# FFN input chunks in pairs by seven half products, and the next layer's tables and modulation in its own phases

## The chip, the cores and the metric

The kernel runs on one core of one Trainium2 chip. The metric is the time of the whole program on the device in microseconds (us), as the median of its runs. A separate execution, taken by the hardware profiler, gives the trace.

## The reference

Two layers of a trunk over 640 tokens (512 latent, 128 context) of width 1024, all float32. Each layer has two halves, of which the second is the one whose products change:

```python
def swiglu(xn, w_ffn_in, w_ffn_out):
    gu = xn @ w_ffn_in
    g, u = gu[..., :D_FF], gu[..., D_FF:]
    return (jax.nn.silu(g) * u) @ w_ffn_out

def layer(x, cond, lp, ctx, rope_cs):
    sh_m, sc_m, g_m, sh_f, sc_f, g_f = modulation(cond, lp['w_ada'], lp['b_ada'])
    xn = rms_norm(x, lp['norm_mix_g']) * (1 + sc_m) + sh_m
    mix, ckv_n, k_pe, ssm_final = mixer(xn, lp, ctx, rope_cs)
    x = x + g_m * mix
    xn = rms_norm(x, lp['norm_ffn_g']) * (1 + sc_f) + sh_f
    x = x + g_f * swiglu(xn, lp['w_ffn_in'], lp['w_ffn_out'])
    return x, ckv_n, k_pe, ssm_final
```

D_FF is 2816, so w_ffn_in is 1024 by 5632. The modulation is silu(cond) @ w_ada + b_ada, six sections of 1024 channels, for two streams (latent and context), and depends on no token. The mixer's state-space branch needs tables (powers, kernels, rotations) that depend only on the layer's parameters.

## The kernel before

**Layout.** Activations stand channel-major: 8 tiles of 128 channels by 640 tokens, in two halves of 320. Every operand of a float32 product is split in a high and a low part (fp32r), and a product is three matmuls: high weights by high activations, low by high, high by low. A chunk of weights is 128 input channels by 8 tiles (kt) of 128 output columns, 512 KB; `weights` loads it (tile `wraw`), ScalarE casts it to `whi` (L319), the vector engine subtracts to make `wlo` (L320). There are three buffers of each of these (`WBUFS`), and loads and splits are put 400 instructions ahead in priority.

**Stages of a layer.** `mixer_in` (input projection, attention, Fourier, convolution), `mixer_out` (state-space branch and gated merges; its last results are the tiles `acc`, split into `xh` and `xl`), and `tail`: the output projection with the residual and the norm, then the FFN. In the FFN a tile f of 128 hidden channels takes a gate chunk and an input chunk (in the code `wfi[f]` and `wfi[NF+f]`, NF = 22), each 8 x 3 x 2 = 48 matmuls of 320 columns, all by `mm` (L238). Silu of the gate is on ScalarE (L1521), the multiplication with the other chunk on the vector engine (L1523), and the result f_s is split in `hh` and `hl`. FFN_ROUNDS cuts the 22 tiles in rounds of 8, 8 and 6; after each round 8 output chunks (`wfo`) add its part to the residual (L1332). The last three chunks of the last round go by halves of the tokens, so that the norm (squares at L433) can start early. One further tile of the next round stands ahead of each output projection.

**Layer 1's work in layer 0.** During `tail` of layer 0 two side chains run: `layer_tables` (the state-space tables of layer 1, then the rotations) and `modulations` of all six sections of layer 1. The latter reads each 512 KB of `w_ada` with the vector engine, two operations of 1024 columns (one for each stream, L572) for a tile. For layer 0 itself the tables are made in `mixer_in`, the rotations beside its attention, and four sections of its modulation in `mixer_out`.

**Order.** TensorE's order is fixed when the program is written: a main stream of products, and between them the steps of side chains, each put where an estimated clock (`now`) says that it is ready. The other engines' orders come from a scheduler with priorities; `issue_after(anchor)` ties the modulation's operations to the main stream's progress on the vector engine. Sums are collected in PSUM: the tile `main` has two buffers of two banks, one bank for each half of the tokens.

Of the kernel before, what the change touches and what calls it, by code (L numbers as in the profile page):

```python
# [9 lines left out]
F32 = mybir.dt.float32  # L10
# [30 lines left out]
TABLES_PACE = (1.5, 3.0)  # L41
TABLES_START = 80.0
ROT_START, ROT_PACE = 8.0, 6.0
MOD_START = (12.0, 90.0)
MOD_PACE = (10.5, 7.0)
# [5 lines left out]
# ---------------------------------------------------------------- host layout  # L51
# [12 lines left out]
def _constants():  # L64
# [17 lines left out]
    # the DFT over the latent positions p = 8k + s: sums and differences of the positions p and -p come in (those of  # L82
    # 0 and 256 share a place), a half of the positions goes out, the even ones first
# [16 lines left out]
    # the sum over four 32-row blocks of the rotary key, and of its swap  # L100
# [27 lines left out]
    # the first two sections of the first layer: piece t holds the tiles t of both,  # L128
    # [half of the channels, channel, 4 x 2 x 128]; the others: [channel of the section, channel]
# [75 lines left out]
# ---------------------------------------------------------------- the program  # L205
class Program:
    def __init__(self, tc, A, O, taps=None):
        self.tc, self.nc, self.A, self.O, self.taps = tc, tc.nc, A, O, taps or {}
        self.n = 0
        self.now = 0.0             # estimated time of the tensor engine, in ns  # L210
        self.ntags = (("hh", 9), ("hl", 9))
# [3 lines left out]
        self.spare = 0             # chunks of weights to come that the vector engine has no time for  # L215
        self.anchor = None         # the last step of the main stream on the vector engine
        self.slots = [[False, 0.0] for _ in range(2)]

# [12 lines left out]
    # -- the order of the tensor engine: a main stream of products, and between its parts the  # L231
    # steps of side chains, each put where its operands are expected to be ready
# [11 lines left out]
    def side(self, gen, urgent=False, behind=False):  # L244
        """Starts a side chain: a generator that yields the time (us) until its next step is ready."""
# [16 lines left out]
    def tick(self):  # L262
        """Runs the side steps that are ready."""
# [74 lines left out]
    def main_ps(self):  # L338
        return self.t(self.ps, [128, 2, 512], "main", bufs=2)
# [1263 lines left out]
```

## Time and profile before

| what | value |
|---|---|
| median of 3 runs | 2672.55 us (2671.49 to 2681.19) |
| span of the profiled execution | 2683.6 us |
| TensorE busy | 2618.7 us (98%) |
| vector engine (DVE) busy | 1534.2 us (57%) |
| ScalarE (ACT) busy | 883.2 us (33%) |
| GpSimd (POOL) busy | 187.9 us (7%) |
| chain that ended last | TensorE 84%, issue 9%, vector engine, ScalarE and DMA 2% each |

Busy shares are of the span. The chain is followed back from the last instruction: at each step to what released it. PE is TensorE, PEld its loading of weights, SP the engine that issues most loads. PEclk is the granted clock of TensorE, 1.00 being 2.4 GHz and 0.50 being 1.2 GHz.

### The profile page before, as it was taken

What the parts mean: (1) busy time and instruction counts of PE and PEld (TensorE: products, weight loads), DVE (VectorE), ACT (ScalarE), POOL (GpSimd) and SP (SyncE); (2) the same over time, 40 slices, a digit from 0 to 9 for tenths busy, and PEclk for the clock granted to TensorE, in tenths of its full rate; (3) what the DMA queues carried; (4) which work ended last, traced back from release to release, by engine and by line L of the source; (5) the groups of instructions that cost most, each with busy time, mean ns of one, the idle gap of its engine ahead of it and who ended that gap; (6) DMA issues with size and microseconds to landing.
All of it is one profiled execution on the core that took longest, in us unless ns stands there. A gap on an engine that the chain in (4) does not pass through costs nothing.

```text
span 2683.6 us, 44723 instructions
## 1 busy us (share of the span) xinstructions
PE 2618.7 (98%) x18518; PEld 2505.7 (93%) x18518; DVE 1534.2 (57%) x3061; ACT 883.2 (33%) x1393; POOL 187.9 (7%) x316
## 2 busy tenths in 40 slices
PE   7999999999999999999999899999999999999999
PEld 5987898999999899999979779999999999999999
DVE  5888764776557579989453356654454444232323
ACT  5334544233224422221243244433323233212211
POOL 0110000111001100000020000011100010000000
PEclk8999999999999999999999999999999999999999
DMA  6442115574435255655232221155532322222222
GB/s 250 135 150 85 56 61 173 176 216 140 126 121 172 63 165 181 202 179 166 80 119 75 60 63 52 50 155 160 149 99 80 107 74 71 79 72 79 71 75 75
DMA packets 118747, 312.78 MB, mean 117 GB/s; under 512 B 35344, under 2 KB 46160, under 8 KB 118288
## 3 DMA queue, kind: packets, MB, share of 16 engines
q1 hardware_dynamic: 99376, 250.52, 30.7%
q0 software_dynamic: 16432, 55.39, 6.1%
q10 hardware_dynamic: 2736, 4.01, 0.4%
q8 instruction: 146, 2.39, 0.4%
q14 instruction: 57, 0.47, 0.1%
HBM read 267.07 MB, written 42.80 MB: 115 GB/s over the span
## 4 chain that ended last, share of the span: by engine, by line
PE 84%; issue 9%; DVE 2%; ACT 2%; DMA 2%; POOL 0%; ACTq 0%; SPq 0%; DVEq 0%; POOLq 0%
PE main L238 74%; PE side L238 9%; PE side L242 1%; DMA s_EF<-d_et 1%; DVE xl L463 1%; DVE wlo L320 0%; ACT whi L319 0%; ACT pq L897 0%; DVE hl L458 0%; ACT P L794 0%; DMA yb<-d_br 0%; POOL d_r L1136 0%; DVE hh L458 0%; DVE sm L791 0%; ACT xh L461 0%
## 5 line engine op out<-in xcount | busy, mean ns | idle before, releaser
L238 PE MATMUL main<-xh,whi 128*128 128x320 f32 x3488 | 831.2, 315 | 1.7 <-ACT xh L461 1.3
L238 PE MATMUL main<-xl,whi 128*128 128x320 f32 x3488 | 815.8, 311 | 1.7 <-DVE xl L463 1.5
L238 PE MATMUL main<-xh,wlo 128*128 128x320 f32 x3488 | 813.5, 310 | 0.0
L319 ACT CAST whi<-wraw 128x1024 fp32r<-128x1024 f32 (+1 forms) x302 | 312.3, 1034 | 1162.4 <-PE main L238 675.9
L238 PEld LDWEIGHTS main<-xh,whi 128*128 128x128 f32 x3488 | 585.7, 189 | 25.1 <-issue 19.9
L238 PEld LDWEIGHTS main<-xl,whi 128*128 128x128 f32 x3488 | 590.4, 189 | 6.7 <-DVE xl L463 6.4
L320 DVE TENSOR_TENSOR wlo<-wraw,whi 128x1024 fp32r<-128x1024 f32 (+1 forms) x302 | 367.7, 1218 | 397.0 <-ACT whi L319 395.7
L238 PEld LDWEIGHTS main<-xh,wlo 128*128 128x128 f32 x3488 | 590.5, 189 | 0.0
L238 PE MATMUL main<-yb,whi 128*128 128x320 f32 x1152 | 231.3, 312 | 2.1 <-ACT yb L319 2.1
L572 DVE SCALAR_TENSOR_TENSOR ada_j<-ada,ada_c 128x1024 bf16<-128x1024 f32 x160 | 195.1, 1219 | 3.8 <-DMA ada<-wada 2.9
L238 PEld LDWEIGHTS main<-yb,whi 128*128 128x128 f32 x1152 | 184.7, 189 | 3.0 <-ACT yb L319 2.4
L1332 DVE SCALAR_TENSOR_TENSOR x<-main,ada,x 128x320 f32<-128x320 f32 (+2 forms) x192 | 75.6, 434 | 177.2 <-PE main L238 176.9
L238 PE MATMUL main<-hh,whi 128*128 128x320 f32 x704 | 167.4, 311 | 0.0
L238 PE MATMUL main<-hh,wlo 128*128 128x320 f32 x704 | 166.2, 309 | 0.0
L238 PE MATMUL main<-hl,whi 128*128 128x320 f32 x704 | 166.2, 309 | 0.0
L238 PE MATMUL main<-yb,wlo 128*128 128x320 f32 x576 | 131.9, 310 | 0.0
L1523 DVE TENSOR_TENSOR f_s<-main,f_s 128x640 f32<-128x640 f32 x44 | 36.2, 824 | 150.6 <-PE main L238 150.6
L238 PEld LDWEIGHTS main<-hh,whi 128*128 128x128 f32 x704 | 119.0, 188 | 3.5 <-issue 3.5
L238 PEld LDWEIGHTS main<-hh,wlo 128*128 128x128 f32 x704 | 119.2, 188 | 0.0
L238 PEld LDWEIGHTS main<-hl,whi 128*128 128x128 f32 x704 | 119.2, 188 | 0.0
L238 PEld LDWEIGHTS main<-yb,wlo 128*128 128x128 f32 x576 | 97.1, 189 | 0.0
L794 ACT ACTIVATE P<-side,sm,rq 128x640 f32<-128x640 f32 (+1 forms) x80 | 63.9, 800 | 98.7 <-DVE sm L792 97.0
(320 smaller groups left out, 2761.3 us busy)
## 6 DMA issues: line engine op xcount, KB each, us to landing
ada<-wada SPq DMA_DIRECT2D x96, 512.0 KB, 4.4
wraw<-wfi SPq DMA_DIRECT2D x88, 512.0 KB, 3.6
wraw<-wgate SPq DMA_DIRECT2D x64, 512.0 KB, 3.6
wraw<-win SPq DMA_DIRECT2D x50, 512.0 KB, 3.7
wraw<-wbr SPq DMA_DIRECT2D x32, 512.0 KB, 3.7
wraw<-wfo SPq DMA_DIRECT2D x32, 512.0 KB, 3.6
d_f<-t_G POOLq DMA_DIRECT2D x16, 512.0 KB, 4.1
d_et<-t_et POOLq DMA_DIRECT2D x16, 512.0 KB, 5.1
```

The costliest lines, as they stand in the source:

```text
L238: self.nc.tensor.matmul(out, lhsT, rhs, **kw)
L242: self.nc.tensor.transpose(out, in_, ident)
L319: self.nc.scalar.copy(out=hi, in_=src)
L320: self.nc.vector.tensor_sub(out=lo, in0=src, in1=hi.bitcast(F32))
L463: nc.vector.scalar_tensor_tensor(out=xl[:, a:b], in0=t[:, a:b], scalar=B[:, s:s + 1], in1=xh.bitcast(F32)[:, a:b], op0=ALU.add, op1=ALU.su ...
L572: nc.vector.scalar_tensor_tensor(out=junk, in0=w, scalar=1.0, in1=sc[:, s, :], op0=ALU.mult, op1=ALU.mult, accum_out=self.ada[l][:, o + t, ...
L794: nc.scalar.activation(out=p[:, :nk].rearrange("p (a b) -> p a b", a=s.shape[1]), in_=s, func=AF.Exp, scale=rq, bias=small[:, 1:2], accum_ ...
L1332: self.anchor = nc.vector.scalar_tensor_tensor(out=x[:, o:o + n], in0=p, scalar=gcol[:, s:s + 1], in1=x[:, o:o + n], op0=ALU.mult, op1=ALU ...
L1523: self.anchor = nc.vector.tensor_mul(out=two(s), in0=pu[:, :, :HALF], in1=two(s))
```

## The change

**Pairs.** The tiles f = 0 and 1 of each layer stay as they were. From f = 2 on (`PLAIN`) the gate chunk and the input chunk are computed together as a 2 x 2 product: columns gate and input, channels in two halves of four tiles (kt), tokens in two halves. In place of eight half products there are seven (Strassen's scheme in Winograd's form), of 4 x 3 = 12 matmuls each. Four of them take sums of weight halves, made for each pair on the vector engine in `wsum` and then split, and four take sums of activations, T1 to T4, made once per layer by `sums` after f = 0 from copies of the normed tiles (tiles `bs`), T1 being written over an operand by `place` at f = 2. A pair takes four `whi` and four `wlo` buffers (seven halves of 512 columns), still out of three. The order is P1, P2, P5, U2, P3, P4, U3 in banks a, b, c, a, c, d, a; U2, P3 and U3 add to what stands in their bank. ScalarE copies P1, P5, U2 and the negative of P4 out; the vector engine adds the gate halves (P2, P3) ahead of Silu, adds U3 to both input halves, and multiplies (L1636 of the changed file).

**Rounds and buffers.** The rounds are 6, 6, 6 and 4 tiles, so four output projections in place of three; `hh` and `hl` have seven buffers in place of nine. `main` is one tile of four banks, taken in turn.

**Moves.** `layer_tables` goes: the tables of layer 1 are made in `mixer_in` of layer 1, its rotations beside its attention, and four of its sections of modulation in its `mixer_out`, as for layer 0. Only two sections stay in `tail` of layer 0, with one buffer in place of two and a pace of 12 in place of 7.

The diff, cut to its core (comments are gone from the changed file too, which moves its line numbers):

```diff
-FFN_ROUNDS = [(0, 8), (8, 16), (16, 22)]
+FFN_ROUNDS = [(0, 6), (6, 12), (12, 18), (18, 22)]
+PLAIN = 2
...
-        self.ntags = (("hh", 9), ("hl", 9))
+        self.ntags = (("hh", 7), ("hl", 7))
...
     def main_ps(self):
-        return self.t(self.ps, [128, 2, 512], "main", bufs=2)
+        self.bank = (self.bank + 1) // 2 * 2 % 4
+        ps = self.mainps[:, self.bank:self.bank + 2, :]
+        self.bank = (self.bank + 2) % 4
+        return ps
+    def strassen_weights(self, first, second, ahead=AHEAD):
...
+            raw = [self.t(wp, [128, 1024], "wraw", bufs=WBUFS) for _ in range(2)]
+            for r, d in zip(raw, (first, second)):
+                nc.sync.dma_start(out=r[:, :n], in_=d.rearrange("p k m -> p (k m)"))
+            hi, lo = [], []
+
+            def pair(parts):
+                h = self.t(wp, [128, 1024], "whi", F32R, bufs=WBUFS)
+                l = self.t(wp, [128, 1024], "wlo", F32R, bufs=WBUFS)
+                o = 0
+                for p in parts:
+                    k = p.shape[1]
+                    self.split(h[:, o:o + k], l[:, o:o + k], p)
+                    for i in range(k // m):
+                        out.append((h, l, o + m * i))
+                    o += k
+            out = []
+            a, b = raw
+            pair([a[:, :n]])
+            sa, sb = [self.t(self.sp, [128, 1024], "wsum", bufs=2) for _ in range(2)]
+            V.tensor_add(out=sa[:, :m], in0=b[:, :m], in1=b[:, m:n])
+            V.tensor_add(out=sa[:, m:n], in0=sa[:, :m], in1=a[:, :m])
+            pair([sa[:, :n]])
+            V.tensor_add(out=sb[:, :m], in0=sa[:, m:n], in1=a[:, m:n])
+            pair([sb[:, :m], b[:, m:n]])
+            V.tensor_add(out=sb[:, m:n], in0=a[:, :m], in1=b[:, :m])
+            pair([sb[:, m:n]])
+        return out
+
+    def strassen(self, first, second, forms, use):
+        ws = self.strassen_weights(first, second)
+        a, b, c, d = [self.mainps[:, (self.bank + i) % 4, :HALF] for i in range(4)]
+        self.bank = (self.bank + 1) % 4
+        n = first.shape[1] // 2
+        for i, (bank, x, step, start) in enumerate((
+                (a, "B11", "P1", True), (b, "B21", "P2", True), (c, "T1", "P5", True), (a, "T2", "U2", False),
+                (c, "B22", "P3", False), (d, "T4", "P4", True), (a, "T3", "U3", False))):
+            hi, lo, o = ws[i]
+            for k in range(n):
+                xh, xl = forms[x][k]
+                for t, (ww, xx) in enumerate(((hi, xh), (lo, xh), (hi, xl))):
+                    self.mm(bank, ww[:, o + 128 * k:o + 128 * k + 128], xx, start=start and k == 0 and t == 0,
+                            stop=k == n - 1 and t == 2, skip_group_check=not start)
+                self.tick()
+            use(step, bank)
...
+    def sums(self, pool, tags, bs, B, xs):
...
+        for k in range(KD):
+            for a, b, s in ((0, LAT, 0), (LAT, NT, 1)):
+                nc.scalar.activation(out=bs[k][:, a:b], in_=bs[k][:, a:b], func=AF.Identity, bias=B[:, k, s:s + 1])
...
+            V.tensor_sub(out=t1, in0=b11, in1=b12)
+            V.scalar_tensor_tensor(out=t24[:, :HALF], in0=t1, scalar=-1.0, in1=b22, op0=ALU.mult, op1=ALU.subtract)
+            V.tensor_sub(out=t3[:, o], in0=b22, in1=b12)
+            V.tensor_add(out=t24[:, HALF:], in0=t24[:, :HALF], in1=b21)
...
+        def place():
+            for k in range(n):
+                hi, lo = forms["T1"][k]
+                self.split(hi, lo, t1s[k // 2][:, k % 2 * HALF:k % 2 * HALF + HALF])
...
+                if l > 0:
+                    self.tables = self.side(self.ssm_tables(tables, l, TABLES_PACE))
...
-                    if l == 0:
-                        self.rots = self.side(self.rotations(
-                            l, lambda: self.t(pc, [128, 1024], "rotations", bufs=2), ROT_PACE, ROT_START))
+                    self.rots = self.side(self.rotations(
+                        l, lambda: self.t(pc, [128, 1024], "rotations", bufs=2), ROT_PACE, ROT_START))
...
-            if l == 0:
-                self.modulations(p, 0, range(2, 6), MOD_START[0], MOD_PACE[0], 1)
+            self.modulations(p, l, range(2, 6), MOD_START[0], MOD_PACE[0], 1)
...
-                self.tables = self.side(self.layer_tables(pt, l + 1, TABLES_PACE[1]))
-                self.modulations(pt, l + 1, range(6), MOD_START[1], MOD_PACE[1], 2)
+                self.modulations(pt, l + 1, range(2), MOD_START[1], MOD_PACE[1], 1)
...
+            def halves(f):
...
+                def use(step, ps):
+                    if step in ("P1", "U2", "P5"):
+                        nc.scalar.copy(out={"P1": s0, "U2": s1, "P5": u1}[step], in_=ps)
+                    elif step == "P4":
+                        nc.scalar.activation(out=u0, in_=ps, func=AF.Copy, scale=-1.0)
+                    elif step == "U3":
+                        self.anchor = V.tensor_tensor(out=two(u), in0=ps.unsqueeze(1).to_broadcast([128, 2, HALF]),
+                                                      in1=two(u), op=ALU.add)
+                    else:
+                        o = s0 if step == "P2" else s1
+                        V.tensor_add(out=o, in0=ps, in1=o)
+                        nc.scalar.activation(out=o, in_=o, func=AF.Silu)
+                self.strassen(A["wfi"][l, f], A["wfi"][l, NF + f], forms, use)
+                V.scalar_tensor_tensor(out=s, in0=u, scalar=-1.0, in1=s, op0=ALU.mult, op1=ALU.mult)
+                split_h(f, s)
```

Vector engine in the FFN of layer 1, before: `wlo` is a chunk's low part, f_s a tile's gate values and then its result, `hl` the result's low part.

```order
L320 TENSOR_TENSOR wlo_25021<-wraw_25018,whi_25020 128x1024
L1523 TENSOR_TENSOR f_s_24899<-main_24907,f_s_24899 128x640
L320 TENSOR_TENSOR wlo_25081<-wraw_25078,whi_25080 128x1024
L320 TENSOR_TENSOR hl_24958<-f_s_24899,hh_24957 128x640
L320 TENSOR_TENSOR wlo_25138<-wraw_25135,whi_25137 128x1024
L1523 TENSOR_TENSOR f_s_25016<-main_25024,f_s_25016 128x640
L320 TENSOR_TENSOR wlo_25198<-wraw_25195,whi_25197 128x1024
L320 TENSOR_TENSOR hl_25075<-f_s_25016,hh_25074 128x640
```

The same engine and stage now, over a little more than half of a pair; `wsum` is a sum of weight halves, f_u the input half of the result, and the higher numbers belong to the pair that follows.

```order
L1633 TENSOR_TENSOR f_s_22328<-main,f_s_22328 128x320
L321 TENSOR_TENSOR wlo_22471<-wsum_22466,whi_22470 128x1024
L373 TENSOR_TENSOR wsum_22594<-wraw_22587 128x512
L374 TENSOR_TENSOR wsum_22594<-wsum_22594,wraw_22586 128x512
L1629 TENSOR_TENSOR f_u_22329<-main,f_u_22329 128x640
L321 TENSOR_TENSOR wlo_22476<-wsum_22467,whi_22475 128x512
L321 TENSOR_TENSOR wlo_22476<-wraw_22459,whi_22475 128x512
L1636 SCALAR_TENSOR_TENSOR f_s_22328<-f_u_22329,f_s_22328 128x640
L321 TENSOR_TENSOR hl_22453<-f_s_22328,hh_22452 128x640
L1633 TENSOR_TENSOR f_s_22456<-main,f_s_22456 128x320
```

Four operations per tile have become fourteen; the next pair's weight sums stand ahead of a pair's last add, and its first gate add (the last row) stands behind the split of the pair before.

ScalarE in the same place before: casts of weights (`whi`), Silu, cast of the result (`hh`).

```order
L319 CAST whi_25020<-wraw_25018 128x1024
L1521 ACTIVATE f_s_24899<-main_24850 128x640
L319 CAST whi_25080<-wraw_25078 128x1024
L319 CAST hh_24957<-f_s_24899 128x640
L319 CAST whi_25137<-wraw_25135 128x1024
L1521 ACTIVATE f_s_25016<-main_24967 128x640
L319 CAST whi_25197<-wraw_25195 128x1024
L319 CAST hh_25074<-f_s_25016 128x640
```

ScalarE there now: between these stand copies out of PSUM (the COPY rows, and the first ACTIVATE of f_u, the negative of P4), and Silu is in two halves.

```order
L1634 ACTIVATE f_s_22328<-f_s_22328 128x320
L320 CAST whi_22470<-wsum_22466 128x1024
L1627 ACTIVATE f_u_22329<-main 128x320
L320 CAST whi_22475<-wsum_22467 128x512
L320 CAST whi_22475<-wraw_22459 128x512
L1625 COPY f_s_22456<-main 128x320
L320 CAST hh_22452<-f_s_22328 128x640
L320 CAST whi_22482<-wsum_22467 128x512
L1634 ACTIVATE f_s_22456<-f_s_22456 128x320
L1625 COPY f_u_22457<-main 128x320
```

The copy of P5 (the last row) stands behind Silu of P2 (the row ahead of it), and that behind the cast of the tile before.

The vector engine now at a pair of layer 0 beside which a tile of modulation runs; `ada_j` and `ada_c` are that tile's scratch and the condition.

```order
L1629 TENSOR_TENSOR f_u_9237<-main,f_u_9237 128x640
L321 TENSOR_TENSOR wlo_9386<-wsum_9377,whi_9385 128x512
L321 TENSOR_TENSOR wlo_9386<-wraw_9369,whi_9385 128x512
L1636 SCALAR_TENSOR_TENSOR f_s_9236<-f_u_9237,f_s_9236 128x640
L678 SCALAR_TENSOR_TENSOR ada_j_8299,ada_88<-ada_9318,ada_c_8296 128x1024
L321 TENSOR_TENSOR hl_9363<-f_s_9236,hh_9362 128x640
L678 SCALAR_TENSOR_TENSOR ada_j_8299,ada_88<-ada_9318,ada_c_8296 128x1024
L321 TENSOR_TENSOR wlo_9393<-wsum_9377,whi_9392 128x512
L1633 TENSOR_TENSOR f_s_9366<-main,f_s_9366 128x320
L376 TENSOR_TENSOR wsum_9509<-wsum_9508,wraw_9500 128x512
```

The two operations of 1024 columns (L678, before L572) stand around the subtraction of the pair's result, ahead of the next pair's gate add.

## Rows read from the trace of the kernel before

**Rows 1.** The page's part 1: busy us, share, instructions of each engine.

```profile
PE 2618.7 (98%) x18518; PEld 2505.7 (93%) x18518; DVE 1534.2 (57%) x3061; ACT 883.2 (33%) x1393; POOL 187.9 (7%) x316
```

**Rows 2.** Stretches: us, busy us of each engine, PEclk, DMA share, GB/s.

```profile
core 0: us, PE busy (x) PEld busy (x) DVE busy (x) ACT busy (x) POOL busy (x), PEclk, DMA share, GB/s
925.00:1340.00 415.00, 415.00 (x3061) 411.80 (x3060) 329.06 (x707) 100.64 (x134) 23.55 (x37) 1.00 0.51 159
2245.00:2640.00 395.00, 395.00 (x2696) 395.00 (x2695) 117.67 (x146) 83.42 (x97) 0.00 (x0) 1.00 0.25 74
```

**Rows 3.** Timeline, TensorE near the end: start us, us, then the instruction.

```profile
2674.43 0.31 PE L238 MATMUL main<-hl,whi 128*128 128x320 f32 x1
...
2676.48 0.31 PE L238 MATMUL main<-hh,wlo 128*128 128x320 f32 x1
```

**Rows 4.** Timeline of ScalarE and the vector engine at 2609 us.

```profile
2609.70 1.05 ACT L319 CAST whi<-wraw 128x1024 fp32r<-128x1024 f32 x1 [5.39 <-issue]
2610.79 1.23 DVE L320 TENSOR_TENSOR wlo<-wraw,whi 128x1024 fp32r<-128x1024 f32 x1 [0.24 <-ACT whi L319]
2611.93 0.82 DVE L320 TENSOR_TENSOR hl<-f_s,hh 128x640 fp32r<-128x640 f32 x1
```

**Rows 5.** Groups by shape: count, busy us, mean ns, idle time before them.

```profile
L1000 DVE TENSOR_TENSOR t_E<-t_tmp,t_tmp 128x512 f32<-128x512 f32 x16 | 11.0, 688 | 0.5
L1332 DVE SCALAR_TENSOR_TENSOR x<-main,ada,x 128x320 f32<-128x320 f32 x64 | 35.1, 548 | 164.0 <-PE main L238 163.8
L572 DVE SCALAR_TENSOR_TENSOR ada_j<-ada,ada_c 128x1024 bf16<-128x1024 f32 x160 | 195.1, 1219 | 3.8 <-DMA ada<-wada 2.9
L319 ACT CAST hh<-f_s 128x640 fp32r<-128x640 f32 x44 | 31.9, 725 | 4.6 <-DVE f_s L1523 4.4
L433 ACT ACTIVATE hl<-x 128x320 f32<-128x320 f32 x12 | 5.6, 470 | 15.5 <-DVE x L1332 15.5
L1464 ACT COPY ct<-main 128x320 f32<-128x320 f32 x8 | 3.4, 419 | 0.0
```

**Rows 6.** The page's part 6: loads, KB each, median us to landing.

```profile
wraw<-wfi SPq DMA_DIRECT2D x88, 512.0 KB, 3.6
```

**Rows 7.** Tiles P, acc, f_s by layer: min/median/max ns, first to last start.

```profile
L794 ACT ACTIVATE P<-side,sm,rq x40: 457/885/894, 255.5 to 419.1; 128x640 f32<-128x640 f32 x32, 128x128 f32<-128x128 f32 x8
...
L794 ACT ACTIVATE P<-side,sm,rq x40: 457/885/895, 1588.6 to 1751.8; 128x640 f32<-128x640 f32 x32, 128x128 f32<-128x128 f32 x8
...
L320 DVE TENSOR_TENSOR xl<-acc,xh x8: 821/822/825, 815.4 to 829.5; 128x640 fp32r<-128x640 f32 x8
...
L320 DVE TENSOR_TENSOR xl<-acc,xh x8: 818/823/826, 2134.8 to 2148.9; 128x640 fp32r<-128x640 f32 x8
...
L320 DVE TENSOR_TENSOR hl<-f_s,hh x22: 812/819/822, 914.0 to 1333.6; 128x640 fp32r<-128x640 f32 x22
...
L320 DVE TENSOR_TENSOR hl<-f_s,hh x22: 812/818/820, 2233.4 to 2639.6; 128x640 fp32r<-128x640 f32 x22
```

**Rows 8.** Timeline, TensorE at the rotary key of either layer.

```profile
60.82 0.76 PE L238 MATMUL main<-xh,wraw 128*32 128x320 f32 x4 [3.26 <-ACT at L600]
...
1403.62 1.28 PE L238 MATMUL main<-xh,wraw 128*32 128x320 f32 x16 [1.78 <-ACT at L600]
```

**Rows 9.** TensorE behind three gaps (timeline), and the stretches behind them.

```profile
441.47 0.57 PE L238 MATMUL main<-yb,whi 128*128 128x320 f32 x2 [2.11 <-ACT yb L319]
...
610.38 0.90 PE L238 MATMUL side<-s_u,s_EF 128*128 128x80 f32 x3 [3.43 <-DMA s_EF<-d_et]
...
1546.75 0.42 PE L238 MATMUL main<-at,whi 128*128 128x320 f32 x1 [1.33 <-ACT v L701]
...
442.00:446.00 4.00, 4.00 (x18) 3.74 (x17) 2.15 (x4) 1.29 (x3) 0.00 (x0) 0.57 1.08 228
608.00:620.00 12.00, 9.62 (x44) 9.65 (x45) 2.06 (x2) 5.85 (x18) 4.22 (x8) 0.57 0.36 85
1542.00:1560.00 18.00, 16.66 (x95) 12.87 (x94) 9.32 (x14) 6.99 (x11) 0.00 (x0) 1.00 0.30 88
```

More of the change, by code (lines that the diff above doesn't have):

```diff
@@ L217, in __init__ @@
         self.slots = [[False, 0.0] for _ in range(2)]
+        self.bank = 0
     def nm(self, s):
@@ L338, in main_ps @@
     def main_ps(self):
-        return self.t(self.ps, [128, 2, 512], "main", bufs=2)
+        self.bank = (self.bank + 1) // 2 * 2 % 4
[3 more added lines that the diff above has]
+    def strassen_weights(self, first, second, ahead=AHEAD):
+        nc, wp = self.nc, self.wp
+        n = first.shape[1] * first.shape[2]
+        m = n // 2
+        V = nc.vector
+        with self.tc.high_priority(offset=ahead):
+            raw = [self.t(wp, [128, 1024], "wraw", bufs=WBUFS) for _ in range(2)]
[24 more added lines that the diff above has]
+        return out
@@ L482, in operand @@
             def operand(k):
[L483 removed]
+                if keep is not None and len(keep) < KD:
+                    keep.append(self.t(pool, [128, NT], tags[k % 2][0], bufs=tags[k % 2][1]))
+                self.operand(pool, tags[k % 2], x[k], xs[k], A[:, k], B[:, k], r, o, parts, keep and keep[k])
                 if k == KD - 1:
@@ L1398, in start @@
             if t == 4:
-                self.tables = self.side(self.ssm_tables(tables, 0, TABLES_PACE[0]))
+                self.tables = self.side(self.ssm_tables(tables, 0, TABLES_PACE))
             for c in range(2):
@@ L1511, in tail, with split_h @@
                                   [use(d) for d in range(KD - BY_HALVES, KD)])
+            self.sp = p
+            bs = []
             xs, first = self.normed(p, norm, x, self.scale_cols(l, 1), self.ada[l][:, 24:32, :],
-                                    [A["wfi"][l, 0], A["wfi"][l, NF]], self.ntags, func=AF.Silu)
+                                    [A["wfi"][l, 0], A["wfi"][l, NF]], self.ntags, func=AF.Silu, keep=bs)
             two = lambda ap: ap.rearrange("p (a b) -> p a b", a=2)
+            forms, place = None, None
             hs = [None] * NF
-            def ffn_in(f):
+            def halves(f):
+                V = nc.vector
+                s, u = [self.t(p, [128, NT], n, bufs=2) for n in ("f_s", "f_u")]
+                s0, s1, u0, u1 = [x[:, o:o + HALF] for x in (s, u) for o in (0, HALF)]
+                def use(step, ps):
[13 more added lines that the diff above has]
+                split_h(f, s)
+            def split_h(f, s):
+                hi = self.t(p, [128, NT], "hh", F32R, bufs=7)
+                lo = self.t(p, [128, NT], "hl", F32R, bufs=7)
+                self.split(hi, lo, s)
+                hs[f] = (hi, lo)
+            def ffn_in(f):
+                nonlocal forms, place
+                if f >= PLAIN:
+                    if f == PLAIN:
+                        place()
+                    return halves(f)
                 pg = self.chunk(A["wfi"][l, f], KD, xs) if f else first[0]
@@ L1523, in ffn_in @@
                 self.anchor = nc.vector.tensor_mul(out=two(s), in0=pu[:, :, :HALF], in1=two(s))
-                hi = self.t(p, [128, NT], "hh", F32R, bufs=9)
-                lo = self.t(p, [128, NT], "hl", F32R, bufs=9)
-                self.split(hi, lo, s)
-                hs[f] = (hi, lo)
+                split_h(f, s)
+                if f == 0:
+                    forms, place = self.sums(p, self.ntags, bs, self.ada[l][:, 24:32, :], xs)
             nxt = 0
@@ L1531, in tail @@
                 if r == len(FFN_ROUNDS) - 1 and not last:
-                    self.need(self.tables)
                     self.need(self.modside)
@@ L1581, in emit @@
                         self.tap(f"xh{l}_{k}", xs[k][0].bitcast(F32))
-                self.mixer_in(l, xs, first, tables if l == 0 else None)
+                if l > 0:
+                    tables = tc.alloc_tile_pool(name=f"p0t{l}", bufs=2, side="right", reuse_waits="tile")
+                self.mixer_in(l, xs, first, tables)
                 ms = self.mixer_out(l, xs)
```

52 lines of the change are left out of this document (34 added, 18 removed).

## The prediction

> **What bounds the kernel now.** I read the page's busy shares first: TensorE is busy 98% of the span, vector engine and ScalarE far less [rows 1]. The stretches come next: through the FFN of either layer TensorE is busy for every microsecond, at the full clock, while the vector engine has 118 of 395 us in layer 1 and 329 of 415 in layer 0, where the tables and modulation of layer 1 also run [rows 2]. So an FFN lasts as long as its matmuls take one after another, and a matmul removed there is time removed, until another engine becomes late. One matmul of 320 columns starts each 0.1467 us, (2676.48-2674.43)/14, and this in by-halves work, where every matmul has other weights and one bank takes all the sums, as the new products have it [rows 3].
>
> The span is 2683.6 us, 11 above the 2672.55 us median of the timed runs; what lies around the span no row shows. I work out a difference on the profiled execution and add it to the median.
>
> **Removed.** A pair of chunks needs 7 x 4 x 3 = 84 matmuls in place of 8 x 4 x 3 = 96. Twenty pairs in each layer: 480 x 0.1467 = 70.4 us off TensorE. The Trainium skill (TensorE: Matmul & The Clock Gate, Back-to-back issue gap) gives a warm gap of N/2.4 ns plus 2.5, an estimate of 135.8 ns for 320 columns and 65.2 us for the 480; the trace's 146.7 ns disagrees and is used.
>
> **Added inside a pair.** Weight halves are summed and split by vector engine and ScalarE, and seven results are put together. The buffers for split weights stay three, but a pair takes four, so the second of a pair is written only when the sixth product of the pair before has ended. From there one chain runs to the fifth product of the next pair. Its durations, where neighbours on one engine overlap by 0.08 (2610.79+1.23 is 2612.02, the next starts at 2611.93: 0.09, taken as 0.08) and a handover takes 0.04 (2609.70+1.05 to 2610.79) [rows 4]:
> cast 1.05+0.04, subtraction 1.22-0.08 [rows 4]; two sums of 512 columns that depend on each other, 0.69 each [rows 5]; U3 add of 640, 0.74; two subtractions of 512, half of 1.23 or 0.60 each; the product 0.82+0.04; cast of the result 0.73+0.04; its subtraction 0.74 [rows 4, 5]; P2 add of 320 columns about 0.50+0.04 (two operands; with three it is 0.55); Silu 0.47, of which 0.40 to the next start; copy of P5 out of its bank 0.42+0.04 [rows 5]; then products five and six, 2 x 1.76, and 0.20 for the last matmul's tail (its record lasts 0.31, the pitch is 0.147) and handover.
> Sum: 1.09+1.14+1.38+0.74+1.20+0.86+0.77+0.74+0.54+0.40+0.46+3.72 = 13.04 us. TensorE's own work is 84 x 0.1467 = 12.32, so it waits 0.72 us per pair, ahead of P3: that product adds to the bank of P5, ScalarE must have copied P5, and the copy stands in ScalarE's queue behind the Silu of P2, which waits for an add that stands behind the previous pair's product and subtraction. Bounds: 0 if the chain is covered, 0.72+9 x 0.08 = 1.44 if neighbours don't overlap. I take 0.8, nearest to the chain from rows.
>
> A second loop is nearly as long: the raw second chunk is loaded when the subtraction of its buffer's last user is over, 3.6 us at the median [rows 6], then sums, adds, product, result and the next subtraction, about 9.2 us more: 12.8. A landing at 4.4 us makes it 13.6.
>
> The Trainium skill (Perfetto Trace Analysis, Matmuls) says that independent groups should rotate through PSUM banks, so that one is emptied while the next is computed. [...] The trace agrees where keys are made: 1.33 us of waiting for ScalarE's copy of v [rows 9].
>
> The first pair after an output projection has its weights early and waits for nothing, so 16 of 20 pairs count (bursts of 5, 6, 6, 3). Layer 1: 16 x 0.8 = 12.8 us.
>
> Layer 0 has modulation tiles beside 8 of them. Each puts two operations of 1.22 us (start to start 1.15) into the chain on the vector engine [rows 5], one beside the result's cast, and the late subtraction of the pair moves ahead of the P2 add: 13.04-0.12-0.77+2 x 1.15+0.60 = 15.05, waiting 2.7. I take 2.8: 8 x 2.8 = 22.4, and 8 x 0.8 = 6.4. Bounds for these: 8 x 1.4 if the modulation fits into waits, 8 x 3.5.
>
> **The clock.** After an isolated gap of 2.11 us TensorE ran at a mean granted 0.57 in 442-446, after one of 3.43 us at 0.57 in 608-620, that is at 1.2 of 2.4 GHz for most of it; with repeated gaps of 1.33 it kept 1.00 [rows 9]. Gaps of 2.7 lie on the wrong side. At half clock up to two products of the chain cost 3.5 more, but the next gap shrinks as TensorE is slower. I take 1 us per pair, 8 in all; bounds 0 and 28.
>
> **Around the pairs.** Forming the operands costs the vector engine, from the end of the first chunk on: 16 operations of 320 columns at 0.45, six splits of 640 at 0.74, three of the last four splits at 0.45, two weight subtractions 1.14, two sums 0.60, multiplication and result 0.74 each: 18.0 us; then multiplication, 1.20, 0.74 and the last T1 split 0.45: 21.1. The fourth step of P5 wants it at 2 x 7.04+3.52+1.32 = 18.9: 2.2 us late. The biases for these operands stand between the casts of the norm on ScalarE: 2 us more. 4 per layer, 8; bounds 0 and 16.
> The last round has four tiles, so the last result is wanted 3 x 0.88 = 2.64 us after the round starts and comes after 4.6 (add, a weight split, product, cast, subtraction): 2 per layer, 4. Layer 0's norm chain has three half chunks of 1.76 us beside it where it had 2.64: 2 us.
> A fourth round adds 8 residuals and loads per layer; the vector engine has 2.2 us in an output chunk of 5.3: hidden, about 1 us if that cover went.
>
> **Moved.** Layers differ in just this work, so the trace prices it. Tail 0 (end of the merges to the last result): 1333.6-829.5 = 504.1; tail 1: 2639.6-2148.9 = 490.7. Without tables layer 0 loses 13.4 [rows 7]. Input phase (rotary key to first softmax): 255.5-60.8 = 194.7 with tables, 1588.6-1403.6 = 185.0 without; softmaxes 163.6 and 163.2, rotations are hidden [rows 7, 8]. I charge 10. Mixer output: 829.5-419.1 = 410.4 with modulation, 2148.9-1751.8 = 397.1 without [rows 7]; 13.3, but the 3.43 us for s_EF and its slow clock are about 8 of it [rows 9] and need not come again: I charge 9 (0 to 14). Net +5.6.
>
> **Sum:** -70.4+12.8+22.4+6.4+8+8+4+2+5.6 = -1.2 us, so 2671 us. The gain goes into waits within the pairs and moved work.
>
> **Rivals.**
> Covered waits: the vector engine has about 9.4 us in a pair of 12.3, so an order that never leaves P5's copy behind would run at TensorE's pace. For it: under 80% load. Against it: the chain is dependence and queue order, not load. Plain pairs wait for nothing, modulated ones 1.5, no clock loss: -70.4+12+8+4+2+5.6 = -39, 2634 us. Chance 0.27.
> Slow clock and late raw chunks: gaps above 2 us halve the clock at each modulated pair, 28 in place of 8, and landings of 4.4 us make the other 24 later pairs 0.6 longer, 14: +33, 2706 us, slower than before. It decides once a gap exceeds 2.1 us (clock) or a landing 3.8 us. For it: the two clock rows. Against it: repeated gaps of 1.33 left the clock alone, and the loads' median is 3.6. Chance 0.22.
> That products in one bank with ever new weights run slower is ruled out by the by-halves rows [rows 3].
>
> **Chances.** Forecast 0.51, own range 2655 to 2690. Measurement tells 0.5%, 13 us, from no change: below 2659 lie the first rival and 0.10 of the forecast, 0.37; above 2686 lie 0.20 of the second and 0.06 of the forecast, 0.26; between them 0.37. The range for eight in ten reaches into both rivals and leaves out some 0.09 of each: 2630 to 2707.
>
> **What would show it.** In the FFN of layer 1, pairs of about 13.1 us, TensorE waiting 0.7 to 1.4 us for ScalarE's copy f_u ahead of the fifth product; in layer 0 eight pairs of 15 to 16 with gaps near 2.7 and a granted clock below 1.00 behind them. Tail 1 some 16 us shorter, tail 0 about 3, the input phase and mixer output of layer 1 each 9 or 10 longer. I am wrong if pairs run at 12.3 (then faster), if clock falls in layer 1's FFN (then slower), or if the moved tables and modulation cost layer 1 nothing.

## The result, and the profile after

3673.29 us, the median of 4 runs (3665.59 to 3675.89), against 2672.02 before: a ratio of 1.374 (1.371 to 1.377), 1001 us slower. The forecast was 2671, the range 2630 to 2707. The change was meant for the FFN; the trace says that every stage of the program grew.

The page's part 1 and its part 2 for TensorE, of the changed kernel:

```profile
span 3669.4 us, 44837 instructions
PE 2861.6 (78%) x18038; PEld 2603.1 (71%) x18038; DVE 1831.2 (50%) x3577; ACT 1057.4 (29%) x1785; POOL 189.4 (5%) x316
PE   7878987887787676767778689878877877767676
...
PEclk8989988889999988999899889988999999999999
```

TensorE has 480 matmuls fewer, as reckoned, and is busy 78% of the span where it was 98% [rows 1]. It is idle 808 us, where it was 65; busy time grew too, by 243 us. No other engine took its place: the vector engine is down to 50%, and GpSimd and ScalarE are lower still. So most of the time went into waits. The view of waits, TensorE alone, longest sums first (us in total, times, longest):

```profile
PE main L239 <- DVE x L1432: 150.5, 91, 3.0
PE main L239 <- ACT m_s L1385: 127.1, 60, 3.5
PE main L239 <- ACT f_s L1625: 78.9, 80, 1.6
PE main L239 <- DVE f_s L1633: 60.1, 80, 1.8
PE main L239 <- ACT f_u L1627: 58.8, 40, 1.5
PE main L239 <- DVE m_s L1412: 53.3, 48, 2.8
PE main L239 <- DVE f_u L1629: 41.9, 40, 1.1
PE main L239 <- ACT v L807: 34.1, 12, 3.7
...
PE main L239 <- ACT f_u L1625: 20.6, 40, 0.5
```

All name the tile `main`, and the releasers are instructions that read it: the residual's add, the merges (m_s), the copies of a pair. Waits of `main` add up to 768 us in 590 places; before they made 14 us in 13, of which this is the largest sum:

```profile
PE main L238 <- ACT at L600: 5.0, 2, 3.3
```

The counts are the tell-tale: 80 for the copies of P1 and U2 in 40 pairs, 80 for the adds of P2 and P3, 40 each for P4, U3 and P5, so seven waits in every pair. The timeline of one pair, only the rows that waited:

```profile
3029.22 0.41 PE L239 MATMUL main<-xh,whi 128*128 128x320 f32 x1 [0.52 <-ACT f_s L1625]
3031.83 0.42 PE L239 MATMUL main<-xh,whi 128*128 128x320 f32 x1 [0.58 <-DVE f_s L1633]
3034.36 0.41 PE L239 MATMUL main<-th,whi 128*128 128x320 f32 x1 [0.52 <-ACT f_u L1625]
3037.89 0.42 PE L239 MATMUL main<-xh,whi 128*128 128x320 f32 x1 [1.50 <-ACT f_s L1625]
3040.56 0.41 PE L239 MATMUL main<-th,whi 128*128 128x320 f32 x1 [0.65 <-DVE f_s L1633]
3044.11 0.41 PE L239 MATMUL main<-th,whi 128*128 128x320 f32 x1 [1.53 <-ACT f_u L1627]
3047.22 0.42 PE L239 MATMUL main<-xh,whi 128*128 128x320 f32 x1 [1.09 <-DVE f_u L1629]
```

The first row is P2, which goes to bank b. It waits for the copy of P1 out of bank a. P5 in c waits for the add of P2 out of b, and so on to the next P1, which waits for the add of U3: each of the seven waits for the reader of the product just before it, which stands in another bank. Whoever wants the bank itself again (U2 wants a) had its reader done a product ago. A pair takes 20.5 us where its matmuls take 12.3. Whole chunks do the same: the next one starts only when the reader of this one is done, though it goes to the other two banks.

The single operations are what they were: a modulation operation as in [rows 5], a load of weights as in [rows 6] (the page's parts 5 and 6).

```profile
L678 DVE SCALAR_TENSOR_TENSOR ada_j<-ada,ada_c 128x1024 bf16<-128x1024 f32 x160 | 194.8, 1217 | 3.0 <-DMA ada<-wada 2.6
...
wraw<-wfi SPq DMA_DIRECT2D x88, 512.0 KB, 3.5
```

Stages of the changed kernel by the tiles that answer to [rows 7] (count: min/median/max ns, first to last start):

```profile
L900 ACT ACTIVATE P<-side,sm,rq x40: 457/886/894, 321.6 to 494.8; 128x640 f32<-128x640 f32 x32, 128x128 f32<-128x128 f32 x8
...
L321 DVE TENSOR_TENSOR xl<-acc,xh x8: 818/819/827, 1034.8 to 1055.0; 128x640 fp32r<-128x640 f32 x8
...
L900 ACT ACTIVATE P<-side,sm,rq x40: 457/886/894, 2159.0 to 2332.3; 128x640 f32<-128x640 f32 x32, 128x128 f32<-128x128 f32 x8
...
L321 DVE TENSOR_TENSOR xl<-acc,xh x8: 818/820/826, 2867.0 to 2885.6; 128x640 fp32r<-128x640 f32 x8
```

The merges of layer 0 end at 1055.0 us in place of 829.5: 225 us are lost before any pair has run and before any moved work is due. In the mixer output of layer 1 it is 553.3 (2332.3 to 2885.6) where it was 397.1, a loss of 156 us. Only one part of the change acts in all these places: `main` is one tile of four banks.

The granted clock has a smaller part. Its mean over the span, before and after (the view of cores):

```profile
core 0: 2683.6 us, clock 0.988
core 0: 3669.4 us, clock 0.935
```

What was not granted makes 32 us of the span before and 239 after, so an estimate of up to 206 us, a fifth of the loss, goes to slow clock, as far as TensorE had work just then. Its busy time shows it too: 243 us more, though 70 us of matmuls are gone (what a start after a gap costs, in the last section, is also in that). The slow clock came with the waits: with the accumulators apart, below, the mean is 0.989. Pairs of layer 0 with modulation beside them, FFN pairs of layer 1, then a stretch of an output projection (us, busy us by engine, PEclk, DMA share, GB/s):

```profile
1195.00:1285.00 90.00, 60.60 (x334) 53.09 (x333) 43.22 (x63) 26.66 (x46) 0.00 (x0) 0.92 0.21 64
...
3009.00:3111.00 102.00, 71.16 (x426) 62.22 (x426) 46.43 (x63) 33.20 (x58) 0.00 (x0) 1.00 0.17 51
3120.00:3190.00 70.00, 52.49 (x295) 49.39 (x295) 23.02 (x40) 9.79 (x14) 0.00 (x0) 0.88 0.15 44
```

Gaps of 0.5 to 1.5 us seven times in a pair left it at 1.00 in layer 1, with TensorE busy 70%; in layer 0, where the longest gap of a pair is 1.8 us, it is 0.92; gaps of 1.3 to 2.5 us between output chunks went with 0.88 in the mean.

### The profile page after: what moved, and what is told of

Its sections match the earlier page's. It is cut to its first block, busy times and chain, and to the rows that moved or that the text cites. A ratio compares the mean times of both kernels' runs of the same rounds, so it can differ in the third digit from the quotient of the medians.

```text
span 3669.4 us, 44837 instructions
## 1 busy us (share of the span) xinstructions
PE 2861.6 (78%) x18038; PEld 2603.1 (71%) x18038; DVE 1831.2 (50%) x3577; ACT 1057.4 (29%) x1785; POOL 189.4 (5%) x316
## 5 line engine op out<-in xcount | busy, mean ns | idle before, releaser
L239 PEld LDWEIGHTS main<-xh,whi 128*128 128x128 f32 x2848 | 506.1, 196 | 444.3 <-ACT f_s L1625 101.0
L320 ACT CAST whi<-wraw 128x1024 fp32r<-128x1024 f32 (+2 forms) x318 | 296.2, 931 | 1280.8 <-PE main L239 1036.8
L321 DVE TENSOR_TENSOR wlo<-wraw,whi 128x1024 fp32r<-128x1024 f32 (+2 forms) x318 | 347.0, 1091 | 498.4 <-ACT whi L320 496.7
L239 PEld LDWEIGHTS main<-xl,whi 128*128 128x128 f32 x2848 | 515.3, 196 | 6.7 <-DVE xl L526 5.4
L239 PE MATMUL main<-hh,whi 128*128 128x320 f32 x704 | 185.4, 342 | 118.4 <-DVE x L1432 110.5
L239 PE MATMUL main<-th,whi 128*128 128x320 f32 x480 | 164.1, 342 | 105.6 <-ACT f_u L1627 58.8
L678 DVE SCALAR_TENSOR_TENSOR ada_j<-ada,ada_c 128x1024 bf16<-128x1024 f32 x160 | 194.8, 1217 | 3.0 <-DMA ada<-wada 2.6
L239 PEld LDWEIGHTS main<-th,whi 128*128 128x128 f32 x480 | 92.7, 193 | 138.4 <-ACT f_u L1627 69.5
L320 ACT CAST whi<-wsum 128x512 fp32r<-128x512 f32 (+1 forms) x120 | 91.2, 760 | 272.1 <-PE main L239 272.1
L321 DVE TENSOR_TENSOR wlo<-wsum,whi 128x512 fp32r<-128x512 f32 (+1 forms) x120 | 104.0, 866 | 112.0 <-ACT whi L320 109.9
L239 PE MATMUL main<-tl,whi 128*128 128x320 f32 x480 | 151.4, 315 | 0.0
L239 PE MATMUL main<-th,wlo 128*128 128x320 f32 x480 | 151.1, 315 | 0.0
```

Of the source, the lines that this page charges most:

```text
L239: self.nc.tensor.matmul(out, lhsT, rhs, **kw)
L320: self.nc.scalar.copy(out=hi, in_=src)
L321: self.nc.vector.tensor_sub(out=lo, in0=src, in1=hi.bitcast(F32))
L678: nc.vector.scalar_tensor_tensor(out=junk, in0=w, scalar=1.0, in1=sc[:, s, :], op0=ALU.mult, op1=ALU.mult, accum_out=self.ada[l][:, o + t, ...
```

## Experiments

**Only the tile.** The kernel before, and of the change one thing.

```diff
-        self.ps = pool("ps", bufs=2, space=PSUM)
+        self.ps = pool("ps", bufs=1, space=PSUM)
+        self.mainps = self.ps.tile([128, 4, 512], F32, name="main", tag="main")
...
-        return self.t(self.ps, [128, 2, 512], "main", bufs=2)
+        self.bank = (self.bank + 2) % 4
+        return self.mainps[:, self.bank:self.bank + 2, :]
```

> The kernel before, with nothing of the change but its accumulator: one tile `main` of four banks for the whole program, taken two banks at a time, in place of two tiles of two banks. Theory 1 (a product waits for the last read of the tile, whatever bank that read is of): 40 pairs of the changed kernel lose about 8.3 us each (a pair lasts 20.6 us, its matmuls 12.3), 333 us; the other 736 us that it lies above 2672 - 70 are lost by whole chunks. Here 80 more whole chunks stand in the place of the pairs and lose some 2 us each, 160: about 2672 + 736 + 160 - 30 (the fourth rounds) = 3540 us, between 3350 and 3650. Theory 2 (it is the pairs: a bank taken again after one product, and their chains on the other engines): no pairs here, so 2672 us within 13.

3412.31 us (3407.09 to 3418.48), ratio 1.277 (1.275 to 1.280). Theory 1 holds: 740 of the 1001 us come with the tile alone, without a pair or a moved table. The loss per whole FFN tile was a little smaller than I had assumed: 17.37 us where 14.08 are due, so 1.6 us per chunk. Its timeline, the rows of TensorE that waited in the FFN of layer 1:

```profile
2917.29 0.56 PE L239 MATMUL main<-xh,whi 128*128 128x320 f32 x2 [0.99 <-DVE f_s L1526]
2926.37 0.56 PE L239 MATMUL main<-xh,whi 128*128 128x320 f32 x2 [1.78 <-ACT f_s L1524]
2934.66 0.56 PE L239 MATMUL main<-xh,whi 128*128 128x320 f32 x2 [0.99 <-DVE f_s L1526]
```

Each chunk waits for the reader of the chunk before (Silu, then the multiplication), in the other two banks.

**Two tiles that stand as long.** The kernel before, with a standing tile for each two banks.

```diff
+        self.mainps = [self.ps.tile([128, 2, 512], F32, name=f"main{i}", tag=f"main{i}") for i in range(2)]
...
+        self.bank = 1 - self.bank
+        return self.mainps[self.bank]
```

> The kernel before, with two tiles of two banks that stand for the whole program, taken in turn, in place of tiles that are handed out anew for each chunk. Theory 1 (waits follow the tile, and here a chunk's tile was read a whole chunk ago): 2672 us within 13. Rival (it is not the tile's size but that a tile stands for the whole program and its place is never given back): as slow as with one tile, 3350 us or more.

2671.22 us, ratio 0.999 (0.998 to 1.001). That the tile is never handed back costs nothing; that products and readers of different banks share it costs 740 us.

**The pairs on two standing tiles.** The whole change, the four banks as two tiles of two.

```diff
-        a, b, c, d = [self.mainps[:, (self.bank + i) % 4, :HALF] for i in range(4)]
+        a, b, c, d = [self.mainps[(self.bank + i) % 4 // 2][:, (self.bank + i) % 2, :HALF] for i in range(4)]
```

> The whole change, but its one tile of four banks is two tiles of two banks that stand for the whole program; nothing else. Whole chunks alternate between the tiles and wait for nothing. In the pairs, by the order of their banks, 2 and 3 by turns of the seven products follow a product in the same tile: P2 and P4, then P1, P5 and U3. In the changed kernel the products start 2.53, 2.68, 2.55, 3.53, 2.68, 3.56 and 3.11 us apart where 1.76 are due (P2, P5, U2, P3, P4, U3, next P1), so these five waits cost 0.77 + 0.92 and 1.35 + 0.92 + 1.80, 2.9 us per pair as a mean, 115 for 40 pairs. Theory 1 (a wait for each product that follows one in its own tile, and for no other): e_fix less its 20 us at the take-overs, plus 115, 2740 us, 2700 to 2775, with pairs of 14 and 16.4 us by turns. Rival (pairs that share any tile pay it all): 8.3 us per pair as in the changed kernel, 2957 us.

2763.56 us (2756.3 to 2765.55), ratio 1.034 (1.032 to 1.037), inside theory 1's range and far from the rival's. In two pairs of layer 1 TensorE waited at the five places that I had counted, P2 and P4 of one and P1, P5 and U3 of the next:

```profile
2475.36 0.41 PE L239 MATMUL main<-xh,whi 128*128 128x320 f32 x1 [0.52 <-ACT f_s L1625]
2483.75 0.41 PE L239 MATMUL main<-th,whi 128*128 128x320 f32 x1 [1.09 <-DVE f_s L1633]
2488.97 0.42 PE L239 MATMUL main<-xh,whi 128*128 128x320 f32 x1 [1.43 <-DVE f_u L1629]
2493.40 0.41 PE L239 MATMUL main<-xh,whi 128*128 128x320 f32 x1 [0.64 <-DVE f_s L1633]
2502.00 0.41 PE L239 MATMUL main<-th,whi 128*128 128x320 f32 x1 [1.30 <-ACT f_u L1627]
```

A product waits when it follows one in its own tile, and otherwise not: halving the tile took 910 us off the changed kernel.

**One bank, one tile, for the pairs.** The whole change; the pairs take four tiles of one bank, all other chunks two tiles of two banks as before, in a pool that changes between the two.

```diff
+    def places(self, m):
+        if self.mode != m:
+            if self.mode:
+                self.mp.release()
+            self.mode = m
+            if m:
+                self.mp = self.tc.alloc_tile_pool(name=self.nm("mp"), bufs=1, side="right", space=PSUM, reuse_waits="tile")
+            if m == 4:
+                self.four = [self.t(self.mp, [128, 512], f"four{i}", bufs=1) for i in range(4)]
...
-        a, b, c, d = [self.mainps[:, (self.bank + i) % 4, :HALF] for i in range(4)]
+        self.places(4)
+        a, b, c, d = [self.four[(self.bank + i) % 4][:, :HALF] for i in range(4)]
```

> The whole change, but the sums of the pairs in four tiles of one bank each, and those of all other chunks in two tiles of two banks, as before. Theory 1 (the one tile is the whole loss): what is left is the sum of the prediction, 2671 us, with pairs of about 13.1 us in layer 1, in any case between 2630 and 2707. Theory 2 (a bank taken again after one product, and the chains of the pairs): most of the loss stays, 3300 us or more, with pairs near 20 us.

2645.1 us (2634.36 to 2650.5), ratio 0.989 (0.988 to 0.991): 27 us faster than before, within theory 1's range, and the pairs' waits are gone, also those of 0.8 us that the theory had left in them. Timeline of the vector engine, layer 0, two results with a modulation tile between them, and the stretches of four such pairs and of layer 1:

```profile
1049.00 0.82 DVE L322 TENSOR_TENSOR hl<-f_s,hh 128x640 fp32r<-128x640 f32 x1
...
1051.34 1.21 DVE L687 SCALAR_TENSOR_TENSOR ada_j<-ada,ada_c 128x1024 bf16<-128x1024 f32 x1
...
1061.32 0.82 DVE L322 TENSOR_TENSOR hl<-f_s,hh 128x640 fp32r<-128x640 f32 x1
```

```profile
1049.00:1098.00 49.00, 49.00 (x336) 49.00 (x335) 46.80 (x72) 27.45 (x49) 0.00 (x0) 1.00 0.39 123
2245.00:2605.00 360.00, 353.98 (x2397) 352.75 (x2396) 225.47 (x347) 145.38 (x244) 0.00 (x0) 1.00 0.25 78
```

12.32 us from result to result, 84 x 0.1467 to the hundredth, at full clock, even where the vector engine is busy 46.8 of 49 us. The same 12.32 stands between results of layer 1.

**The order that the prediction reckoned with.** In the kernel with a tile for each bank the scheduler put ScalarE's copy of P5 (the first row, of its timeline) ahead of Silu of P2 (the second); in the changed kernel it stands behind, as the order rows with the change show.

```profile
2373.78 0.43 ACT L1634 COPY f_u<-four 128x320 f32<-128x320 f32 x1 [0.46 <-PE four L240]
...
2376.54 0.46 ACT L1643 ACTIVATE f_s<-f_s 128x320 f32<-128x320 f32 x1
```

Bound back to the place behind it:

```diff
-                        nc.scalar.copy(out={"P1": s0, "U2": s1, "P5": u1}[step], in_=ps)
+                        with tc.issue_after(silu[-1].ins) if step == "P5" else nullcontext():
+                            nc.scalar.copy(out={"P1": s0, "U2": s1, "P5": u1}[step], in_=ps)
```

> As e_fix, but ScalarE's copy of P5 is bound behind Silu of P2, the order that the changed kernel has on ScalarE and that the prediction's chain rests on (in e_fix the scheduler put the copy ahead of that Silu, and pairs run at 12.32 us). Theory 1 (the chain of the prediction was right for that order): the later pairs of each round, 16 in each layer, wait 0.7 to 1.4 us for the copy, 13.0 to 13.8 us long: 2645 + 32 x 0.8 = 2671 us, 2660 to 2695. Rival (the chain is covered in any order): pairs of 12.3 us, 2645 within 8.

2717.33 us (2713.84 to 2723.84), ratio 1.018 (1.016 to 1.019), 72 us above the kernel with the other order. The wait is the one named, ahead of P3 for the copy f_u, but each is 1.86 us, not 0.7 to 1.4. This is not quite the order of the changed kernel: the cast of a whole chunk stands ahead of Silu as well. The view of waits for it; its timeline (TensorE, the vector engine's add of P2, then the cast and Silu on ScalarE); and the four us before and after the waits:

```profile
PE four L240 <- ACT f_u L1635: 44.7, 24, 1.9
...
2403.05 0.41 PE L240 MATMUL four<-xh,whi 128*128 128x320 f32 x1 [1.86 <-ACT f_u L1635]
2419.03 0.41 PE L240 MATMUL four<-xh,whi 128*128 128x320 f32 x1 [1.86 <-ACT f_u L1635]
...
2401.12 0.48 DVE L1643 TENSOR_TENSOR f_s<-four,f_s 128x320 f32<-128x320 f32 x1
...
2401.27 1.04 ACT L321 CAST whi<-wraw 128x1024 fp32r<-128x1024 f32 x1 [2.26 <-issue]
2402.22 0.47 ACT L1644 ACTIVATE f_s<-f_s 128x320 f32<-128x320 f32 x1
```

```profile
2399.00:2403.00 4.00, 2.19 (x15) 1.93 (x14) 3.26 (x6) 1.74 (x5) 0.00 (x0) 1.00 0.15 62
2403.00:2407.00 4.00, 3.95 (x17) 3.95 (x18) 1.07 (x2) 0.78 (x2) 0.00 (x0) 0.61 0.39 131
...
2419.00:2423.00 4.00, 3.97 (x27) 3.97 (x28) 1.05 (x2) 0.87 (x3) 0.00 (x0) 1.00 0.43 131
```

The add was done at 2401.60 and Silu began at 2402.22, so an estimate of 0.6 us of the wait is the cast's, and 1.2 the chain's own. After one gap the clock fell to 0.61 in the mean of four us and that pair took 15.98 us; after the next, equal one it stayed at 1.00 and the pair took 14.45. Both theories missed: the chain is not covered in that order, and it costs 72 us where I had 26. Only 24 of the 32 pairs waited, 44.7 us in all; the rest fits a lower clock (0.979 in the mean against 0.989, an estimate of up to 28 us) and what a start after a gap costs (last section).

**Only the moves.** The kernel before, with the changes of the diff to `mixer_in`, `mixer_out` and the start of `tail`, and no pairs.

```diff
-                self.tables = self.side(self.layer_tables(pt, l + 1, TABLES_PACE[1]))
-                self.modulations(pt, l + 1, range(6), MOD_START[1], MOD_PACE[1], 2)
+                self.modulations(pt, l + 1, range(2), MOD_START[1], MOD_PACE[1], 1)
```

> The kernel before with the moves alone: the tables of layer 1 and four sections of its modulation in its own phases, no pairs, the accumulators as before. The prediction's terms for them give 13.4 less in the tail of layer 0, 10 more in the input phase of layer 1 and 9 more in its mixer output (0 to 14): 2672 + 5.6 = 2678 us, 2665 to 2690. Rival (the work is hidden wherever it stands): 2672 within 3, with the phases of layer 1 no longer than before.

2675.67 us, ratio 1.0008 (0.9994 to 1.0021): within the range, though it can't be told from no change by the time alone. The stages tell it, for layer 1 by these rows:

```profile
L793 ACT ACTIVATE P<-side,sm,rq x40: 457/884/892, 1577.4 to 1740.4; 128x640 f32<-128x640 f32 x32, 128x128 f32<-128x128 f32 x8
L319 DVE TENSOR_TENSOR xl<-acc,xh x8: 821/822/824, 2133.5 to 2147.5; 128x640 fp32r<-128x640 f32 x8
```

The tail of layer 0 is 14.3 us shorter (823.8 to 1313.6), the stretch from there to layer 1's first softmax 8.8 longer (1313.6 to 1577.4, where it was 255.0), the mixer output 10.0 longer (1740.4 to 2147.5). The rival falls.

**Take-overs and the first pairs.** Three further steps on the repaired kernel. First, the new kind of tile begins in the two banks that were not written last:

```diff
+            if m == 2:
+                self.slot = (self.bank - 1) % 4 // 2
+            if m == 4:
+                self.bank = 2 * (1 - self.slot)
```

> As e_fix, but where pairs and whole chunks take over from each other, the first of the new sums goes to the two banks that the last of the old ones is not in. In e_fix the stretches between results that hold an output projection are 2 to 4 us longer than their matmuls (118.4 and 120.4 us for six pairs and 288 matmuls, which make 116.2; 81.1 at the end, where 79.2 are due), in both layers some 20 us. Theory 1 (these are waits for banks read a moment ago): 2645 - 20 = 2625 us, 2612 to 2638. Rival (the output projections wait for the residual's adds or their weights): 2645 within 7.

2652.87 us (2644.5 to 2661.95), ratio 0.993 (0.991 to 0.996): no gain, a little above the rival's 2645 within 7, yet not for its reason. The second and the last round of layer 1 now run at the pace of their matmuls (116.15 us, 118.4 before; 78.8, 81.1 before), and the third got worse, 121.7; the first pair of layer 1, too, came 4.4 us later behind its tile (19.3 in place of 14.9), in a wait of 5.8 us for the multiplication of that tile. Then, on top, `PLAIN = 3`:

> As e_fix2, with three whole tiles ahead of the pairs in each layer in place of two (PLAIN = 3). In e_fix the second tile's result comes 16.7 us after the first and the third's 14.9 us after the second in layer 1, 16.6 and 19.1 in layer 0, where a whole tile's matmuls take 14.1 and a pair's 12.3: some 5 us in layer 1 and 9 in layer 0 go to forming the operands. Theory 1 (the first pair comes too early for its operands): a pair less costs 1.76 per layer, 3.5, the waits go for the most part: 7 to 10 us faster than e_fix2, about 2616. Rival (the vector engine's work there delays whatever follows): 3.5 us slower than e_fix2.

2630.1 us (2625.29 to 2635.11), ratio 0.984 (0.982 to 0.986), 23 us faster than the step before, where I had expected 7 to 10. The third round was slow still, by one wait for a residual's add:

```profile
2444.93 0.38 PE L240 MATMUL four<-xh,whi 128*128 128x320 f32 x1 [2.52 <-DVE x L1447]
```

If the pool gives the two tiles their places by which was asked for first, this take-over began in the banks just written. With the places fixed:

```diff
                 self.slot = (self.bank - 1) % 4 // 2
+                for i in range(2):
+                    self.t(self.mp, [128, 2, 512], f"main{i}", bufs=1)
```

> As e_fix2p3, but the two tiles of the whole chunks are placed in a fixed order, so that the take-over really goes to the two banks that are free. In e_fix2p3 two of the three rounds of layer 1 run at the pace of their matmuls (116.2 and 78.8 us), and one waits 2.5 us for the residual's add of the chunk before and then runs at a granted clock of 0.86 for 12 us: 121.7 us. Theory 1 (there the first pair of the round went to the two banks just written, since the place of each tile follows from which was asked for first): 5.5 us in each layer, 2630 - 11 = 2619 us, 2612 to 2626. Rival (the add itself is late, whatever the bank): 2630 within 6.

2616.03 us (2613.94 to 2618.01), ratio 0.979 (0.978 to 0.981), in theory 1's range. This is the fastest version: 54 us under before, and 1057 under the changed kernel. Its FFN of layer 1:

```profile
2245.00:2590.00 345.00, 344.49 (x2348) 343.96 (x2347) 219.37 (x339) 139.35 (x233) 0.00 (x0) 1.00 0.27 80
```

TensorE idles half a microsecond in 345, as it idled nothing before [rows 2], and the second and third round take 116.2 us each, the last 78.8.

## Why the prediction was wrong

**The step that failed** is in the part on the change: its list of what is added has sums, splits, results, operands, rounds and moves, and nothing for `main`. That the four banks became one tile was given no cost at all; I took the banks of a tile for independent, as two tiles are. The runs put 740 us on that one edit without pairs; with pairs, taking it away alone made 1028 us (3673.29 to 2645.1), more than the whole loss. Where the chain had one wait of 0.72 us in a pair, ahead of P3, the trace has seven, one ahead of each product, and a pair lasts 8.2 us longer than its matmuls. No rival held it. The second theory of the first experiment, a bank taken again after one product, comes nearest; but it would have a product wait for the reader of its own bank, a true dependence, where the trace shows P2 waiting for P1's copy out of another. And it could have been read without a chip: the changed kernel's order on TensorE, with its waits, has this at a pair (P1, then P2). A wait for ScalarE stands on P2, though ScalarE last read P2's bank a pair earlier, for the copy of P5, and U2 of that pair had waited for that copy already:

```
L239 MATMUL main<-xh_21799,whi_25718 128x320 [waits DVE_49]
...
L239 MATMUL main<-xh_21807,whi_25718 128x320 [waits Activation_49]
```

I had read the order for what stands where and not for what waits.

**The other steps**, tested on kernels without that tile:

- 70.4 us off TensorE: right. Pairs of 12.32 us against 14.08 for whole tiles.
- 41.6 us of waits within the pairs (12.8, 22.4 and 6.4): wrong by their condition. They rest on an order of ScalarE that belonged to the one-tile program; for the repaired one the scheduler chose another order, and every pair in steady work, with modulation or without, ran at 12.32. So the second loop, reckoned at 12.8, did not bind there either. With the copy bound behind Silu, the wait came at the place named, 1.86 us long with a cast in it that the chain did not have; 72 us in all, against 26 reckoned.
- 8 us of slow clock: none in the repaired kernel's pairs (1.00), where there were no gaps. In the forced order it came, in some pairs and not in others, behind gaps of 1.86 us, so the 2.1 us that the second rival put as its limit is too high.
- 8 us for the operands: too little. In the repaired kernel the first two steps of the FFN took 6.8 us more than their matmuls and the usual start in layer 1, and 11.0 in layer 0 (results at 906.69, 923.34 and 942.42), 17.8 in both, against 8. A third whole tile, which puts the first pair later, took off 23 us with the places as they were.
- 6 us for the last round and the norm behind it (4 and 2): 4.1. From the last result to the rotary key of layer 1 the repaired kernel takes 59.96 us where it was 70.05 with 14.08 more of matmuls, 4.0 longer; from layer 1's last result to the end 29.98 where it was 43.97, 0.1 longer. The wait for the last result is 0.49 us in each layer, not 2.
- The moves, net +5.6: measured +3.2 (-1.6 to +5.6). By stage -14.3, +8.8 and +10.0 against -13.4, +10 and +9. Pricing moved work by the same work in the other layer was the best step of the prediction.
- "What would show it" used tails that end at the last result. They leave out the last output projection, which shrank from six tiles' matmuls to four's, 14.1 us per layer, so these lengths could not be set side by side as I proposed.

In sum, the rival of covered waits (2634 us) was close to what the change does where each sum has its own tile: 2645, and 2616 with the take-overs and the first pairs mended. That 2645 lies within the range of the forecast is in part luck. The 49.6 us of waits and slow clock in the pairs did not come; the operands cost 9.8 more than reckoned, and the take-overs, for which the prediction had no term, 17.2 (the six stretches with an output projection, against those of the fastest version). With -70.4 for the matmuls, 17.8, 17.2, 4.1 and 3.2 for the moves this makes -28.1, and -27.3 was measured.

## What to carry to other kernels

In these kernels a PSUM tile was the unit in which the framework ordered writers and readers: what should overlap needed a tile of its own, even where its bytes never met. Whether tiles elsewhere go by the same rule no run here shows. When a change merges buffers into one allocation, read the list of waits of the new program on the engine that sets the pace, and look for an instruction that waits for a reader of something it doesn't touch. An order is only as good as the waits it was made under: a chain reckoned from one order need not outlive another edit.

## What the runs showed of the hardware

Gaps seven times in 20.5 us (0.52 to 1.53 us each) left the granted clock at 1.00 in the pairs of layer 1, with TensorE busy 71.16 of 102 us; in pairs of layer 0, whose longest gap is 1.84 us, it was 0.92 (1195 to 1285 us), falling to half behind two of four such gaps. Single gaps of 1.86 us between stretches of full work brought it to 0.61 once, at half for most of four us, and left it at 1.00 the next time. And a gap costs more than its length: the first matmul after it lasts 0.41 us with the next one about 0.25 behind, where 0.31 and 0.147 are usual, so that P2 starts 2.54 us after P1 with 0.52 us of idle time, 0.26 more than 1.76 and the idle time make. Of that some 0.16 is the last matmul's record, which outlasts the usual distance, and 0.10 the later start of the second matmul.
